# A fixed order of 32 experts, and the order of a second attention's weights, in a two-block transformer kernel

## The chip, the cores and the metric

The kernel runs as one program on one core of a Trainium2 chip. The metric is device time in microseconds for one execution of the whole program; times of several executions are given as their median. The core has TensorE (in the profile PE for its matmuls, PEld for its weight loads), VectorE (DVE), ScalarE (ACT), GpSimd (POOL) and SyncE (SP), which here issues nearly all DMAs from one in-order queue. Sixteen DMA engines move the data.

## The reference, cut to what matters

Two transformer blocks over 256 tokens of width 1024, in float32. The first block has a mixer (short convolution, gated delta rule, stick-breaking attention) and a feed-forward layer. The second block is conditioned by a vector c, and ends in a mixture of 32 experts, of which each token takes four:

```python
mod = silu(c) @ w_ada + b_ada                       # 1024 x 6144
sh1, sc1, gt1, sh2, sc2, gt2 = split(mod, 6)
h = rms_norm(x, g_pre_mix) * (1 + sc1) + sh1
dq, dk, dv, nq, nk, nv = split(h @ w_in)            # two attentions
mix = concat(diff_attention(dq, dk, dv), neighbourhood_attention(nq, nk, nv)) @ w_out
x = x + gt1 * rms_norm(mix, g_post_mix)
h2 = rms_norm(x, g_pre_ffn) * (1 + sc2) + sh2
f = moe_ffn(h2, ...)                                # 32 experts, top 4, w1 1024x2048, w2 1024x1024 each
x = x + gt2 * rms_norm(f, g_post_ffn)
```

## The kernel before

**Weights.** The dense weights are 67 slabs of one megabyte, numbered in the order of use; w_ada is 24 more ("a" slabs), eight for each third of the modulation. `WS` merges the two lists: `ADA_AT[j]` says ahead of which dense slab the a slab j is loaded. A slab goes into one of six half buffers (three pairs, `w_pair`); the string `PLACES` names the half for each slab of `WS`. `load_slabs` issues slab n once slab n - 6 and the last holder of its half have been read. A dense slab counts as read when ScalarE and VectorE have split it into a high and a low part (`split`, at most four half slabs ahead of use); an a slab when its four matmuls have been written. When the dense list is at its end, each pair of halves, once both are read, becomes one buffer for an expert slab.

**Second attention.** Its twelve slabs are: values of the differential heads (vd, two slabs), keys and queries of differential heads 0 to 3 (one slab each), values of the neighbourhood heads (vn, two slabs), keys and queries of neighbourhood heads 0 to 3 (one each); w_out has four. A host function `pack` puts them into this order. On the chip the stage is written as generators: `head(i)` for i from 0 to 7 (scores, softmax, transposes, mix with the values), `shifts()` for the small vectors, and `projections2()`, which runs `values("vd")`, `keys(0)` to `keys(7)` and `values("vn")`, then the first six of eight w_out products. A planner, `weave`, takes from each generator what TensorE does next and a cost in us, and so fixes the order of instructions when the program is built; `yield 0, 3.0` lets three us of the planner's time go by. `ada(2)` is the last third of the modulation: eight rounds of matmuls into bank acc00, a copy by ScalarE, four transposes, an addition. `shifts()` computes from it the vectors that scale the router's weights. `values` uses banks acc00 and acc01, `head` uses acc10 and acc11, and the w_out products use all four.

**Experts.** The router's top four give counts; experts 0 and 1 are fixed as ranks 0 and 1, the others are sorted by count, largest first. Rank r has a fixed capacity `CAPS[r]` in tokens: 64 for ranks 0 and 1, 128 for 2 and 3, 96 for 4 to 7, 64 for 8 to 17, 32 for 18 to 31. `ORDER` lists the ranks as they are computed; position p is the p-th entry. An expert is six slabs of two megabytes: four of w1, two of w2. There are ten buffers for them, and `load_m` refills buffers in the order of the loads: load n goes into the buffer of load n - 10, when that one and all ahead of it are released. Position p has loads 6p to 6p + 5.

A capacity is cut into blocks of 64 and 32 tokens: 128 is two of 64, 96 is one of 64 and one of 32. For each block TensorE runs `first_rounds` (w1, L1725; two rounds for a block of 64, one for 32), and then `second` (transposes L1745, w2 at L1768 for 64 and L1763 for 32). Slabs are released by the last block of an expert alone. In between stand the gathering of the next expert's tokens (L1683, L1694, L1709) and the addition of the expert before (`combine`, L1791). The last position takes the expert alone with the closing norm (`finish`) behind it.

```python
def free_m(keys):
    for k in keys:
        del m_slab[k]
        m_freed.add(m_num.pop(k))
    while state["freed"] in m_freed:
        load_m(state["next"], m_pool[state["freed"]])
        state["next"] += 1
        state["freed"] += 1
```

Of the kernel before, what the change touches and what calls it, by code (L numbers as in the profile page):

```python
# [21 lines left out]
P = 128  # L22
# [12 lines left out]
NA = 3  # L35


PLACES = "250134250134250134254012543254301254301254301254301243025432154201534201453120345012345"

TURNS = "FABADACCEG"  # L40
NS = len(TURNS)
# [7 lines left out]

FIRST = 2  # L50
CAPS = [64] * 2 + [128] * 2 + [96] * 4 + [64] * 10 + [32] * 14
ORDER = [0, 1, 8, 18, 9, 2, 26, 10, 3, 27, 11, 4, 28, 12, 5, 19, 13, 6, 29, 14, 7, 20, 15, 30, 21, 16, 22, 17, 23, 24, 25,
         31]


N_DENSE = 67
ADA_AT = [14] * 3 + [20] * 5 + [38, 41, 44, 47] + [-1] * 4 + [54] * 2 + [55] * 2 + [56] * 2 + [57] * 2
WS = [w for i in range(N_DENSE + 1) for w in
      [("a", j) for j in range(24) if ADA_AT[j] == i] + ([("s", i)] if i < N_DENSE else [])]
WS_DENSE = [i for i, w in enumerate(WS) if w[0] == "s"]  # L60
# [106 lines left out]
def kernel(ctx: ExitStack, tc: tile.TileContext, x_in, cols_in, rows_in, const_in, cona_in, conb_in, rpb_in,  # L167
# [82 lines left out]
    def load_all(names):  # L250
        for m in range(NS):
            if TURNS[m] in names:
                load_m(m)
# [26 lines left out]
    def col(name, i=None, n=1):  # L280
        a, b = COLS[name]
        t = cols
        if a >= NKEPT:
            t, a, b = cols_mix[0], a - NKEPT, b - NKEPT
        return t[:, a:b] if i is None else t[:, a + i:a + i + n]
# [97 lines left out]
    with sx:  # L383
# [105 lines left out]
        def ada(i, b=None):  # L489

            b = bank() if b is None else b
            for k in range(KC):
                s = WS_ADA[state["ada"]]
                state["ada"] += 1
                w = s_slab[s].rearrange("p (g n) -> p g n", g=4)
                for g in range(4):
                    nc.tensor.matmul(b[32 * g:32 * (g + 1), :], silc[:, k:k + 1].to_broadcast([P, 32]), w[:, g, :],
                                     start=(k == 0), stop=(k == KC - 1))
                slab_read(s)
                if k < KC - 1:  # L500
                    yield 0.94, 0
            r = hp.tile([P, 512], F32, name="adar", tag="wide")
            nc.scalar.activation(r, b, AF.Copy)
            yield 0.94, 1.0
            t = bank()
            for j in range(4):
                nc.tensor.transpose(t[:, j * P:(j + 1) * P], r[:, j * P:(j + 1) * P], ident)
            nc.vector.tensor_tensor(mod[:, 16 * i:16 * (i + 1)].rearrange("p (g j) -> p j g", g=4),
                                    t.rearrange("p (j g r) -> p j g r", j=4, g=4)[:, :, :, 0],
                                    col("b_ada")[:, 16 * i:16 * (i + 1)].rearrange("p (g j) -> p j g", g=4),  # L510
                                    op=OP.add)
            yield 0.3, 0
# [467 lines left out]
        with ExitStack() as s2:  # L980
# [190 lines left out]
            with ExitStack() as s3:  # L1171
# [32 lines left out]
                def values(name):  # L1204
                    t = act.tile([P, 2, 512], F32, name=name)
                    b = [psa.tile([P, 512], F32, name=f"acc0{c}") for c in range(2)]
                    for s in range(2):
                        us = [[u.rearrange("p (k n) -> p k n", k=2) for u in un] for un in units(2)]
                        for c in range(2):
                            for k in range(4):  # L1210
                                kc = 4 * s + k
                                wh, wl = us[k // 2]
                                tok_mm(lambda c, h: b[c], kc, hTh, hTl, wh[:, k % 2, :], wl[:, k % 2, :], kc == 0,
                                       kc == KC - 1, (c,))
                                if k % 2:
                                    if c and k == 1:
                                        split_ahead(3)
                                    yield flush() + [("p", 1.3)]
                    nc.scalar.activation(t[:, 0, :], b[0], AF.Copy)
                    nc.vector.tensor_copy(t[:, 1, :], b[1])  # L1220
                    vs[name] = t

                def keys(i):
                    while i - count["scores"] >= 3:
                        yield 0, 0.1
                    pair = []
                    for n, s in (("k", 1.0), ("q", 1.0 if i < 4 else 0.125)):
                        b = bank()
                        yield from proj_steps(b)
                        t = wk.tile([P, T], F32, name=n + "2", bufs=3)  # L1230
                        nc.scalar.activation(t, b[:, 0:T], AF.Copy, scale=s)
                        pair.append(t)
                        yield [("p", 0.65)]
                    kq[i] = pair
                    if i in (1, 2):
                        nc.scalar.activation(x[:, i - 1, :], x[:, i - 1, :], AF.Copy, scale=r[:, i - 1, 0:1])
                        yield [("A", 1.06)]
                    if i >= 4:
                        window(i - 4)
                        yield [("V", 1.9)]  # L1240
# [122 lines left out]
                def shifts():  # L1363

                    yield 0, 1.0
                    yield from fill
                    yield 0, 4.0
                    b = bank()
                    for k in range(KC):
                        nc.tensor.matmul(b[:, 0:NE], mod[:, 24 + k:25 + k].to_broadcast([P, P]),  # L1370
                                         col("router")[:, k * NE:(k + 1) * NE], start=(k == 0), stop=(k == KC - 1))
                    nc.vector.tensor_add(brow, b[:, 0:NE], row("b_router"))
                    yield 1.0, 4.0
                    gg = small.tile([P, KC], F32, name="gg")
                    nc.vector.tensor_mul(gg, mod[:, 16:24], col("g_post_mix"))
                    for _ in row_steps(gg, grow, hp.tile([P, 4, P], F32, name="diag", tag="wide")):
                        yield 0, 1.5
                    while "ada" not in vs:
                        yield 0, 0.1
                    nc.vector.tensor_mul(gg2, mod[:, 40:48], col("g_post_ffn"))  # L1380

                    nc.vector.scalar_tensor_tensor(gs, mod[:, 32:40], 1.0, col("g_pre_ffn"), op0=OP.add, op1=OP.mult)
                    wr = col("router").rearrange("p (k e) -> p k e", k=KC)
                    nc.vector.tensor_tensor(wr, wr, gs[:, :, None].to_broadcast([P, KC, NE]), op=OP.mult)
# [2 lines left out]

                def projections2():
                    yield from values("vd")
                    fill = ada(2, psa.tile([P, 512], F32, name="acc00"))  # L1390
                    for i in range(8):
                        if i == 4:
                            yield from fill
                            vs["ada"] = True
                            yield from values("vn")
                        yield from keys(i)
                        if i < 4:
                            yield next(fill)
                            yield next(fill)
                    load_all("B")  # L1400
                    while count["scores"] < 8:
                        yield 0, 0.1
                    acc.extend(new_acc())
                    for kc in range(KC - LAST):
                        while count["joined"] <= kc:
                            yield 0, 0.1
                        if "D" not in pools and (count["turned"] == 8 or kc == KC - LAST - 1):
                            while count["turned"] < 8:
                                yield 0, 0.1
                            s4.close()  # L1410
                            pools["D"] = ctx.enter_context(tc.tile_pool(name="slabsD", bufs=1, side="right",
                                                                        reuse_waits="tile"))
                            load_all("D")
                        wh, wl = unit()
                        tok_mm(lambda c, h: acc[c][h], kc, yTh, yTl, wh, wl, kc == 0, False)
                        yield flush() + [("p", 2.6)]
                    while count["joined"] < KC:
                        yield 0, 0.1
# [585 lines left out]
def pack(inp):  # L2004
# [17 lines left out]
    def ada(i):  # L2022
        return [wa[k * P:(k + 1) * P, 2048 * i:2048 * (i + 1)] for k in range(KC)]
# [10 lines left out]
        return ([rows_k(w2[512 * i:512 * (i + 1), v:v + 512]) for i in range(2)]  # L2034
                + [chunk_cols(w2, (k + h * P, q + h * P)) for h in range(4)])

    S += attn(512, 0, 1024) + attn(2048, 1536, 2560)
    S += by2(f("w_out_2")[0])
    S = {"s": S, "a": ada(0) + ada(1) + ada(2)}
    assert len(S["s"]) == N_DENSE  # L2040
# [60 lines left out]
```

## Time and profile before

| | |
|---|---|
| median of 3 runs | 1496.65 us (1492.77 to 1497.12) |
| the profiled execution | 1493.93 us |
| its span, first to last instruction | 1492.1 us |
| mean granted TensorE clock | 0.969 |
| TensorE matmuls busy | 1370.7 us, 92% of the span |
| expert slabs | 192 loads of 2048 KB |

A busy TensorE is an average over stages with different limits: the expert loads are 192 x 2.097 = 402.7 MB of the 504 MB that are read in all. The span is what the trace shows; the execution's time has 1.8 us more around it.

### The profile page before, as it was taken

What the parts mean: (1) busy time and instruction counts of PE and PEld (TensorE: products, weight loads), DVE (VectorE), ACT (ScalarE), POOL (GpSimd) and SP (SyncE); (2) the same over time, 40 slices, a digit from 0 to 9 for tenths busy, and PEclk for the clock granted to TensorE, in tenths of its full rate; (3) what the DMA queues carried; (4) which work ended last, traced back from release to release, by engine and by line L of the source; (5) the groups of instructions that cost most, each with busy time, mean ns of one, the idle gap of its engine ahead of it and who ended that gap; (6) DMA issues with size and microseconds to landing.
All of it is one profiled execution on the core that took longest, in us unless ns stands there. A gap on an engine that the chain in (4) does not pass through costs nothing.

```text
span 1492.1 us, 21744 instructions
## 1 busy us (share of the span) xinstructions
PE 1370.7 (92%) x8859; PEld 736.1 (49%) x8863; DVE 546.6 (37%) x1258; ACT 455.9 (31%) x979; POOL 55.6 (4%) x31
## 2 busy tenths in 40 slices
PE   7999999999899999999999999999999987887674
PEld 6899789998678753333333333333333322222121
DVE  4755678776757841222122122112112111111112
ACT  5564465555556641111111111112111111101111
POOL 2322010000000000000000000000000000000000
PEclk9999999999999999999999999999999998989887
DMA  8322586656774599999899899999999999999994
GB/s 314 113 92 107 186 330 248 258 200 228 260 277 174 179 390 402 424 427 421 345 429 417 346 427 417 426 426 427 428 427 428 427 427 427 428 427 427 428 427 186
DMA packets 43433, 506.66 MB, mean 340 GB/s; under 512 B 5024, under 2 KB 5280, under 8 KB 6880
## 3 DMA queue, kind: packets, MB, share of 16 engines
q1 hardware_dynamic: 42464, 503.49, 82.5%
q10 hardware_dynamic: 864, 1.72, 0.4%
q8 instruction: 72, 1.18, 0.3%
q14 instruction: 33, 0.27, 0.0%
HBM read 504.14 MB, written 1.05 MB: 339 GB/s over the span
## 4 chain that ended last, share of the span: by engine, by line
PE 74%; DMA 17%; ACT 4%; DVE 3%; issue 1%; POOL 0%; SPq 0%; ACTq 0%; DVEq 0%; POOLq 0%
PE mm L1725 23%; DMA w<-in_we 16%; PE mm L447 15%; PE mm L1768 9%; PE acc L1791 4%; PE mm L1683 3%; PE mm L1763 3%; PE acc L481 3%; PE acc L482 3%; PE acc L483 3%; DMA w<-in_ws 1%; PE mm L824 1%; ACT aT L1746 1%; PE mm L1694 1%; PE mm L1730 1%
## 5 line engine op out<-in xcount | busy, mean ns | idle before, releaser
L1725 PE MATMUL mm<-w,xT 128*64 128x512 f32 (+1 forms) x2432 | 449.4, 642 | 56.3 <-DMA w<-in_we 56.0
L1725 PEld LDWEIGHTS mm<-w,xT 128*64 128x64 f32 (+1 forms) x2432 | 134.1, 131 | 354.2 <-issue 279.6
L1734 DVE TENSOR_SCALAR h<-mm 128x256 f32<-128x256 f32 x58 | 24.6, 425 | 714.8 <-PE mm L1730 714.8
L447 PE MATMUL mm<-hT,u 128*128 128x256 f32 x2064 | 263.5, 287 | 1.4 <-DVE hT L436 0.6
L447 PEld LDWEIGHTS mm<-hT,u 128*128 128x128 f32 x2064 | 254.1, 193 | 12.8 <-issue 8.4
L1735 ACT ACTIVATE a<-h 128x256 f32<-128x256 f32 x58 | 24.2, 417 | 506.0 <-DVE h L1734 506.0
L408 DVE TENSOR_TENSOR u<-w,u 128x1024 fp32r<-128x1024 f32 x115 | 145.5, 1270 | 67.3 <-ACT u L403 67.3
L403 ACT ACTIVATE u<-w 128x1024 fp32r<-128x1024 f32 x134 | 139.9, 1056 | 34.0 <-PE acc L483 23.9
L1768 PE MATMUL mm<-w,aT 128*64 128x512 f32 x640 | 143.2, 600 | 5.3 <-ACT aT L1746 5.3
L1768 PEld LDWEIGHTS mm<-w,aT 128*64 128x64 f32 x640 | 44.5, 138 | 91.2 <-issue 81.0
L1773 ACT ACTIVATE y<-mm 128x512 f32<-128x512 f32 x38 | 22.7, 597 | 208.6 <-PE mm L1768 139.8
L1763 PE MATMUL mm<-w,aT 128*32 128x512 f32 x576 | 65.5, 595 | 9.9 <-ACT aT L1746 9.9
L1683 PE MATMUL mm<-x,S 128*32 128x256 f32 (+1 forms) x448 | 57.4, 463 | 2.5 <-DVE S L1670 2.5
L408 POOL TENSOR_TENSOR u<-w,u 128x1024 fp32r<-128x1024 f32 x19 | 46.8, 2465 | 330.5 <-PE mm L306 201.4
L1063 DVE SCALAR_TENSOR_TENSOR fcv<-mm,cols,fcv 128x255 f32<-128x255 f32 x88 | 42.3, 481 | 22.9 <-ACT fcv L1060 21.4
L1701 ACT ACTIVATE xT<-mm,mod,gs 128x64 f32<-128x64 f32 (+1 forms) x152 | 46.6, 386 | 2.1 <-PE mm L1694 1.5
L1703 DVE TENSOR_SCALAR xT<-mm,gs,mod 128x64 f32<-128x64 f32 (+1 forms) x152 | 38.7, 321 | 3.0 <-PE mm L1694 3.0
L1763 PEld LDWEIGHTS mm<-w,aT 128*32 128x32 f32 x576 | 16.8, 109 | 46.5 <-issue 31.1
L1683 PEld LDWEIGHTS mm<-x,S 128*32 128x32 f32 (+1 forms) x448 | 18.7, 119 | 39.6 <-issue 33.1
L1926 POOL TENSOR_TENSOR fs<-fs,x 128x512 f32<-128x512 f32 x1 | 1.3, 1259 | 946.9 <-ACT fr L314 946.9
L1060 ACT ACTIVATE fcv<-mm,cols 128x256 f32<-128x256 f32 x44 | 20.7, 471 | 50.8 <-PE mm L447 50.8
L481 PE MATMUL acc<-u,gh 128*128 128x512 f32 x88 | 34.9, 397 | 0.0
(546 smaller groups left out, 1374.5 us busy)
## 6 DMA issues: line engine op xcount, KB each, us to landing
w<-in_we SPq DMA_DIRECT2D x192, 2048.0 KB, 23.3
w<-in_ws SPq DMA_DIRECT2D x90, 1024.0 KB, 5.3
nb<-in_rpb SPq DMA_DIRECT2D x4, 512.0 KB, 7.7
x<-in_x SPq DMA_DIRECT2D x2, 512.0 KB, 6.1
w<-in_ws SPq DMA_DIRECT2D x2, 512.0 KB, 7.5
bt<-in_b SPq DMA_DIRECT2D x3, 256.0 KB, 8.5
out<-fs SPq DMA_DIRECT2D x3, 256.0 KB, 2.1
grow<-in_wf ACTq DMA_DIRECT2D x1, 512.0 KB, 4.9
```

The lines of the kernel that those rows point to most:

```text
L403: nc.scalar.activation(hi, raw, AF.Copy)
L408: eng.tensor_tensor(lo, raw, hi, op=OP.subtract)
L447: nc.tensor.matmul(b[:, 0:T], w[:, k, :], h[:, k, :], start=(n == 0), stop=(n == 3 * KC - 1))
L481: nc.tensor.matmul(o, th[:, kc, t], wh[:, w], start=first, stop=False)
L482: nc.tensor.matmul(o, th[:, kc, t], wl[:, w], start=False, stop=False)
L483: nc.tensor.matmul(o, tl[:, kc, t], wh[:, w], start=False, stop=last)
L1683: nc.tensor.matmul(b[p * tb:(p + 1) * tb, 0:n], S[:, c, p * tb:(p + 1) * tb], x[:, c, p * n:(p + 1) * n], start=(c == 0), stop=(c == 1))
L1701: nc.scalar.activation(dst, src, AF.Identity, scale=gs[:, kc:kc + 1], bias=mod[:, 24 + kc:25 + kc])
L1725: nc.tensor.matmul(b[p * tb:(p + 1) * tb, :], xT[:, k, q * tb:(q + 1) * tb], w1(p * nr + rd, kc // 4)[:, kc % 4, :], start=(kc == 0), stop ...
L1763: nc.tensor.matmul(b[p * tb:(p + 1) * tb, :], aT[:, 0, j, p0 * tb:(p0 + 1) * tb], w2(bi)[:, j, h * 512:(h + 1) * 512], start=(bi == 0), st ...
L1768: nc.tensor.matmul(b[p * tb:(p + 1) * tb, :], aT[:, rd, j, p0 * tb:(p0 + 1) * tb], w2(bi)[:, j, p * 512:(p + 1) * 512], start=(bi == 0 and ...
L1791: nc.tensor.matmul(acc[c][h], lhsT, rhs, start=False, stop=False, skip_group_check=True)
```

## The change

Three constants and four lines of the second attention. `ORDER` puts ranks with capacity 32 and 64 in front. Position by position the capacities were 64, 64, 64, 32, 64, 128, 32, 64, 128, 32, 64, 96, 32, 64, 96, 32, 64, 96, 32, 64, 96, 32, 64, 32, 32, 64, 32, 64, 32, 32, 32, 32, and become 64, 64, 32, 32, 64, 64, 64, 32, 128, 32, 32, 32, 96, 32, 64, 64, 96, 32, 96, 32, 64, 32, 96, 64, 64, 32, 128, 32, 32, 64, 64, 32. In the second attention vn comes after `keys(1)` instead of after `keys(3)`; the eight rounds of `ada(2)` come one after each of `keys(2)` to `keys(7)` and two at the end, and its transposes and addition move into `shifts()`, three us of planner's time behind. The a slabs move in the list accordingly. `PLACES` names other halves; up to slab 65 each slab follows the same one as before in its half, only the numbers of the halves differ.

```diff
-PLACES = "250134250134250134254012543254301254301254301254301243025432154201534201453120345012345"
+PLACES = "531240531240531240530125304530412530412530412530412504153045230512340512340521435012345"
-ORDER = [0, 1, 8, 18, 9, 2, 26, 10, 3, 27, 11, 4, 28, 12, 5, 19, 13, 6, 29, 14, 7, 20, 15, 30, 21, 16, 22, 17, 23, 24, 25,
-         31]
+ORDER = [0, 1, 18, 19, 8, 9, 10, 20, 2, 21, 22, 23, 4, 24, 11, 12, 5, 25, 6, 26, 13, 27, 7, 14, 15, 28, 3, 29, 30,
+         16, 17, 31]
-ADA_AT = [14] * 3 + [20] * 5 + [38, 41, 44, 47] + [-1] * 4 + [54] * 2 + [55] * 2 + [56] * 2 + [57] * 2
+ADA_AT = [14] * 3 + [20] * 5 + [38, 41, 44, 47] + [-1] * 4 + [58, 59, 60, 61, 62] + [63] * 3
...
                     while "ada" not in vs:
                         yield 0, 0.1
+                    yield 0, 3.0
+                    yield from vs["ada"]
                     nc.vector.tensor_mul(gg2, mod[:, 40:48], col("g_post_ffn"))
...
                     yield from values("vd")
-                    fill = ada(2, psa.tile([P, 512], F32, name="acc00"))
                     for i in range(8):
-                        if i == 4:
-                            yield from fill
-                            vs["ada"] = True
+                        if i == 2:
                             yield from values("vn")
+                            fill = ada(2, psa.tile([P, 512], F32, name="acc00"))
                         yield from keys(i)
-                        if i < 4:
-                            yield next(fill)
+                        if i >= 2:
                             yield next(fill)
                     load_all("B")
+                    yield next(fill)
+                    next(fill)
+                    yield 0.94, 0.3
+                    vs["ada"] = fill
...
-    S += attn(512, 0, 1024) + attn(2048, 1536, 2560)
+    a1, a2 = attn(512, 0, 1024), attn(2048, 1536, 2560)
+    S += a1[:4] + a2[:2] + a1[4:] + a2[2:]
```

## Rows read from the trace of the kernel before

**Rows 1.** The page's slices: bytes moved, 40 equal parts of the span.

```profile
GB/s 314 113 92 107 186 330 248 258 200 228 260 277 174 179 390 402 424 427 421 345 429 417 346 427 417 426 426 427 428 427 428 427 427 427 428 427 427 428 427 186
```

**Rows 2.** The chain of waits in order of time (start, us, what), its last part.

```profile
1215.75 39.07 DMA w<-in_we
...
1461.98 4.87 PE mm L1725 x25
```

**Rows 3.** Windows: stretch, length, busy per engine, PEclk, DMA share, GB/s.

```profile
700.00:720.00 20.00, 19.75 (x108) 6.89 (x105) 6.32 (x20) 3.64 (x11) 0.00 (x0) 1.00 1.00 419
720.00:740.00 20.00, 19.62 (x118) 6.36 (x118) 0.00 (x0) 2.34 (x5) 0.00 (x0) 1.00 0.69 274
...
800.00:820.00 20.00, 19.75 (x108) 7.03 (x106) 5.12 (x16) 3.22 (x10) 0.00 (x0) 1.00 0.99 410
820.00:840.00 20.00, 19.61 (x130) 6.53 (x126) 1.18 (x3) 3.11 (x8) 0.00 (x0) 1.00 0.69 273
...
880.00:900.00 20.00, 20.00 (x144) 6.63 (x141) 3.30 (x9) 1.22 (x3) 0.00 (x0) 1.00 0.99 407
...
920.00:1460.00 540.00, 471.70 (x2842) 154.92 (x2834) 94.06 (x304) 78.48 (x217) 0.00 (x0) 0.94 1.01 427
```

**Rows 4.** The chain of waits: first w1 matmuls of positions 0, 1, 2, 5, 6, 7, 11, 12.

```profile
547.71 7.09 PE mm L1725 x32
...
580.74 7.02 PE mm L1725 x32
...
607.43 6.87 PE mm L1725 x32
...
685.38 6.87 PE mm L1725 x32
...
735.09 7.00 PE mm L1725 x64
...
751.29 7.02 PE mm L1725 x32
...
877.62 6.87 PE mm L1725 x32
...
916.79 7.00 PE mm L1725 x64
```

**Rows 5.** Expert loads: seventh, 31st, up to the 45th (that one's landing), up to 77th.

```profile
L246 SPq DMA_DIRECT2D w<-in_we x1: 327/327/327, 530.3 to 530.3; - x1
...
DMA to landing us min/median/max: 8.5/8.5/8.5
...
L246 SPq DMA_DIRECT2D w<-in_we x1: 332/332/332, 645.9 to 645.9; - x1
...
DMA to landing us min/median/max: 16.2/16.2/16.2
...
L246 SPq DMA_DIRECT2D w<-in_we x45: 327/333/1222, 389.1 to 730.0; - x45
...
DMA to landing us min/median/max: 9.0/9.0/9.0
...
L246 SPq DMA_DIRECT2D w<-in_we x77: 327/333/1222, 389.1 to 896.3; - x77
```

**Rows 6.** TensorE's waits, 546 to 660: for whom, us in total, times, longest.

```profile
PE mm L1683 <- DVE S L1670: 1.8, 1, 1.8
```

**Rows 7.** Windows of the second attention, columns as in rows 3.

```profile
395.00:531.50 136.50, 130.88 (x855) 105.50 (x854) 91.75 (x189) 79.40 (x188) 2.59 (x1) 0.99 0.64 238
480.00:500.00 20.00, 19.83 (x160) 18.28 (x160) 19.24 (x49) 14.39 (x39) 0.00 (x0) 1.00 0.39 131
```

**Rows 8.** TensorE's waits, 394 to 531.

```profile
PE mm L507 <- ACT adar L503: 4.2, 2, 3.1
```

**Rows 9.** TensorE's timeline at 453.67: the transposes, idle time before them in brackets.

```profile
453.67 0.66 PE L507 MATMUL mm<-cst,adar 128*128 128x128 f32 x4 [1.06 <-ACT adar L503]
```

**Rows 10.** One window, columns as in rows 3.

```profile
1220.00:1250.00 30.00, 21.54 (x116) 5.57 (x120) 3.51 (x12) 3.34 (x9) 0.00 (x0) 0.79 1.01 428
```

## The prediction

> **What bounds the kernel now.** I read the page's slices first: from the fifteenth slice to the last but one 390 to 429 GB/s are moved, but for two dips, to 345 and 346 [rows 1]. The chain of waits, read backwards from the end, is one stretch of expert-slab DMA from 1215.75 to 1461.98 and then a tail of matmuls and vector work; before 1215.75 it runs on TensorE [rows 2]. So two limits follow each other, and what joins them is the slab stream: it has no gap after 920 (540 us at 427 GB/s, [rows 3]), so every microsecond that it lost before then is still missing at the end, although TensorE is idle by then. The windows tell where it lost them. At 427 GB/s a 2,097 KB slab takes 4.91 us; a window's deficit is its length times (427 - rate) / 427. That gives 0.4 us in 700:720, 7.2 in 720:740, 0.8 in 800:820, 7.2 in 820:840 and 0.9 in 880:900, together 16.5 us [rows 3].
>
> Why it lost them: ten buffers are refilled in strict order, so load n waits until slab n - 10 is released. An expert is six slabs, 29.4 us of stream. TensorE's time for one, from its first L1725 group to the next expert's, is 26.7 us for a capacity of 64 (580.74 to 607.43), 49.7 for 128 (685.38 to 735.09), 16.2 for 32 (735.09 to 751.29) and 39.2 for 96 (877.62 to 916.79) [rows 4]. Call lag the time from the landing of an expert's first slab to its first matmul. Against 29.4 us the lag changes by -2.7 for 64, +20.3 for 128, -13.2 for 32 and +9.8 for 96; it can't fall below about zero, where TensorE waits for slabs.
>
> A 128 expert has two blocks and releases slabs only with the second. In position 5 its fifth slab (the 35th of all) was released 44.6 us after its start, when the 45th load was issued at 730.0; that load landed 9.0 us later, so 4.1 us lie between issue and the 4.9 us of transfer [rows 4, 5]. The stream has no gap if this release comes 4.1 us before the fourteenth landing counted from the expert's first, that is 13 x 4.9 - 4.1 = 59.6 us after the first landing. So a 128 expert stalls the stream when it starts with a lag over 59.6 - 44.6 = 15.0 us. Here the first slab landed at 645.9 + 16.2 = 662.1 and the lag was 23.3: a stall of 8.3 by this rule, 7.2 by the window. For a 96 expert the first slab binds: released 896.3 - 877.62 = 18.7 us after the start, limit 9 x 4.9 - 4.1 - 18.7 = 21.3 us [rows 4, 5]. Every stall of the window view sits at a 128 or a 96 that was reached with too much lag.
>
> **The change, part by part.** (1) *Order of ranks.* Work and bytes are the same: every rank once. What moves is the lag. Position 1 starts at 580.74, its first slab having landed at 530.3 + 8.5 = 538.8: lag 41.9 [rows 4, 5]. Positions 0 and 1 stay. Before, only one 32 lies ahead of the first 128, and the lag there is still 23.3. After, positions 2 to 7 hold 32, 32, 64, 64, 64, 32. From 41.9, position 1 takes 2.7, the two 32s 13.2 each, less 3 us that I allow for the routing work which the code puts behind positions 2 and 3 (an estimate: TensorE waited 1.8 us for VectorE there, [rows 6], and has some small matmuls), three 64s 2.7 each and the 32 of position 7 13.2: 41.9 - 2.7 - 26.4 + 3 - 8.1 - 13.2 = -5.5, so zero is reached before position 8, where the first 128 stands. It starts with lag 0; TensorE then is paced by the landings through the first four slabs (18.2 us instead of 14.2), which counts as a lag of 4. Limit 15: 11 us to spare, no stall. After it the lag is 24; a 32 or 64 with one block releases at once, and three 32s bring it to zero. Each later 96 is reached after a 32, or after two 64s behind a 32, with a lag of 0 to 4 against 21; the other 128, position 26, comes after 64, 64 and 32 at zero. So the whole 16.5 us should go. Lower bound of the gain 9 us (one 128 still costs its stall), upper 18.5 (a little more if position 1, which gathers for a 32 next, releases earlier). I take 16.5.
>
> The end: the last expert is rank 31 before and after, and the 30 us behind 1461.98 [rows 2] hang on its fourth slab. The two 64s ahead need 26.7 of 29.4 us, so TensorE waits by then in either order: no cost, hidden by the stream; rival E has what it is without that cover.
>
> (2) *Values early, third modulation late.* The same matmuls, in another order. TensorE is busy 130.88 of the 136.5 us from 395 to 531.5 [rows 7], so the stage is bound by its own matmuls and their sum does not change. It was idle 4.2 us for the transposes of the modulation, waiting for ScalarE's copy, in two places, 3.1 us in the longer one [rows 8]; the 1.06 us one, at 453.67, is that of the third modulation [rows 9]. The new text lets 3 us go by (in the planner's time) ahead of these transposes, so that wait should go: -1.06. The eight rounds of modulation matmuls (0.94 us each in the planner's list), which need nothing of VectorE, now stand between the neighbourhood heads, where VectorE is busy 19.24 of 20 us [rows 7]: some tenths more. Against it, the first output product needs the bank that the modulation held, so it waits for the same ScalarE copy, with exponentials queued ahead of it; behind it on TensorE stand all output products. Bounds: gain at most the 5.6 us of idleness less the 3.1 that stay, 2.5; loss at most one more wait like the longer, 3.1. I take -1.5, nearer to the wait that is seen to go.
>
> (3) *Slots and queue.* The stream is at 0.64 of its capacity in this stage [rows 7], so one-megabyte slabs in another order cost nothing while each is issued a key step ahead. On SP's queue the last modulation slabs now release the first pair, so the second expert load goes out later, behind the output weights; the seventh load lands at 538.8 and the first expert starts at 547.71 [rows 4, 5], so some 9 us cover it. If that cover were gone, the start of the experts would move one for one.
>
> **Sum.** -16.5 - 1.5 = -18.0 us on the span of 1492.1: 1474.1. The profiled execution took 1493.93, 1.8 over its span: 1475.9. The median of the runs, 1496.65, is 2.7 over that execution: **1478.6**, say 1478.5.
>
> **Rivals.** *A, the forecast* (0.74): 1474 to 1483.
>
> *B, stalls come back at other experts* (0.12). TensorE would wait for slabs from position 8 on instead of from 1215, and where it waits like that, in 1220:1250, the granted clock was 0.79 in the mean [rows 10], so for some 42% of the time at the lower level, 1.2 GHz. The Trainium skill's page "TensorE: Matmul & The Clock Gate", section "HAM oscillation — how this bites in real kernels", states that an engine which waits for DMA between bursts begins each burst at half clock; the fall to 0.79 agrees. By the row alone: at 0.79 a 128 takes 49.7 / 0.79 = 62.9 us, 13.2 more, 2 over the 11 to spare; for the two of them 4 us, 1482.5. A clock below that stalls each by up to the 8 of before, and the 96s a little: up to 1493. Against it: a 128 has four rounds without a wait once its first four slabs are there.
>
> *C, the attention loses* (0.08): a wait in front of the output products of 3 to 6 us beyond my value: 1482 to 1487 with the stalls gone.
>
> *D, no effect* (0.03): the stream's dips are the memory's and not the buffers'; 1493 to 1499. Against it: the rule gives their places.
>
> *E, slower* (0.03): the two 64s at positions 29 and 30 fall behind. They run at the end, with nothing to absorb a lag: at clock g they take 26.7 / g, and decide from g = 0.91 on. At 0.79 they take 33.8, 4.4 over each, 9 us in all; it ends slower than before only if g stays near 0.65 through both, 11.7 over each: 1502. No row of this trace is so low over 30 us.
>
> **Chances.** A difference under 0.3% (4.5 us) can't be told from none. A, B's better part and C give faster: 0.92; the rest of B and D same: 0.05; E slower: 0.03. A lies within 1471 to 1487, with C and the lower third of B: about 0.84.
>
> **What would show it.** Right: no window of 20 us between 640 and the last landing below 420 GB/s; TensorE waits for expert slabs from about 740; the last L1725 wait ends 18 us earlier; slab DMA in the chain well before 1215; no wait at L507 in the second attention but the first. Wrong: a dip near 790 to 820 or 1320 to 1350 (the 128s), TensorE still in a 64 when the last slab lands, or an attention stage longer than 136.5 us. The number is wrong by just as much as the first expert starts earlier or later than I have it.

## The result, and the profile after

The changed kernel takes 1477.88 us (median of four runs, 1477.23 to 1479.49) beside 1495.02 us for the kernel before in the same rounds: ratio 0.9889, 95% interval [0.9875, 0.9903], about 17 us faster. Forecast were 1478.5 and "faster". The profiled execution took 1478.14 us, its span is 1476.3 instead of 1492.1, and the mean granted clock is 0.984 instead of 0.969. Lines from the experts' part on carry a number that is three higher than before (L1725 is now L1728, L1683 is L1686, L1768 is L1771).

The page of the kernel after, its slices:

```profile
span 1476.3 us, 21754 instructions
...
PEclk9999999999999999999999999999999999999998
...
GB/s 317 115 87 92 209 321 230 272 215 231 238 151 229 279 352 389 430 427 427 427 428 428 426 427 428 427 429 427 426 428 427 427 428 426 427 428 426 428 429 172
```

The two dips of [rows 1] are gone; from the seventeenth slice on no slice but the last is below 426. Windows of the kernel after, columns as in [rows 3]:

```profile
700.00:720.00 20.00, 19.69 (x108) 6.94 (x106) 6.44 (x22) 3.23 (x10) 0.00 (x0) 1.00 1.00 427
720.00:740.00 20.00, 14.59 (x80) 3.60 (x80) 0.00 (x0) 1.79 (x3) 0.00 (x0) 0.83 1.00 426
...
800.00:820.00 20.00, 19.47 (x166) 6.86 (x166) 3.50 (x12) 3.62 (x10) 0.00 (x0) 1.00 1.01 428
820.00:840.00 20.00, 18.06 (x147) 5.34 (x136) 4.83 (x18) 4.00 (x12) 0.00 (x0) 1.00 1.01 425
880.00:900.00 20.00, 18.59 (x136) 6.47 (x134) 5.12 (x16) 3.23 (x10) 0.00 (x0) 1.00 1.01 427
395.00:531.50 136.50, 131.66 (x856) 105.50 (x855) 92.08 (x190) 80.14 (x189) 2.58 (x1) 0.99 0.63 236
1283.50:1336.60 53.10, 49.04 (x252) 16.91 (x256) 8.32 (x24) 5.95 (x17) 0.00 (x0) 1.00 1.01 428
750.70:803.30 52.60, 49.01 (x256) 16.73 (x256) 8.33 (x24) 6.40 (x17) 0.00 (x0) 1.00 1.01 428
640.00:1450.00 810.00, 731.51 (x4308) 245.73 (x4308) 150.64 (x485) 123.32 (x337) 0.00 (x0) 0.99 1.01 427
```

The two windows that held 274 and 273 GB/s [rows 3] hold 426 and 425, and the stream runs at 427 GB/s for 810 us. 750.70:803.30 and 1283.50:1336.60 are the two experts of capacity 128 (positions 8 and 26). In 720:740 the roles are turned round: the stream is full, and TensorE is idle for 5.4 of 20 us. The chain of waits, in order of time (start, us, what):

```profile
547.59 7.09 PE mm L1728 x32
...
579.16 8.71 PE mm L1728 x32
...
625.77 7.00 PE mm L1728 x64
...
641.80 7.02 PE mm L1728 x32
648.86 37.72 DMA w<-in_we
686.74 38.88 DMA w<-in_we
725.74 39.06 DMA w<-in_we
764.84 3.65 PE mm L1728 x16
...
803.53 6.87 PE mm L1728 x64
811.02 33.62 DMA w<-in_we
844.76 39.07 DMA w<-in_we
...
1368.22 39.03 DMA w<-in_we
1407.37 39.04 DMA w<-in_we
1446.45 4.64 PE mm L1728 x25
```

Before, slab DMA entered the chain in 1215.75 [rows 2]; now it carries it from 648.86, with stretches on TensorE in between (764.84 to 811.02 is the first 128), in which the stream has no gap. The last wait for a slab ends at 1446.45 instead of 1461.98, 15.5 us earlier, and what follows takes 29.8 us instead of 30.1. Nearly all of the 15.8 us on the span lie there. From each load's issue and its time to landing, the 192nd slab lands at 1456.15 instead of 1471.67.

How the first 128 is met, on TensorE's timeline (idle time before in brackets):

```profile
750.72 3.65 PE L1728 MATMUL mm<-w,xT 128*64 128x512 f32 x16
755.05 3.65 PE L1728 MATMUL mm<-w,xT 128*64 128x512 f32 x16 [0.69 <-DMA w<-in_we]
...
760.05 3.65 PE L1728 MATMUL mm<-w,xT 128*64 128x512 f32 x16 [1.12 <-DMA w<-in_we]
764.84 3.65 PE L1728 MATMUL mm<-w,xT 128*64 128x512 f32 x16 [1.14 <-DMA w<-in_we]
```

It is paced by landings through its first four slabs, as forecast, and starts 0.6 us after its first slab (landed 750.1). It releases its fifth slab 48.4 us after its start; from 44.6 and the lag counted as 4 I had 48.6.

What the clock did with the earlier waits, TensorE by form of matmul over the whole expert part, two rows of the kernel after and the second one's counterpart before:

```profile
L1728 PE MATMUL mm<-w,xT 128*64 128x512 f32 x1280 | 288.8, 598 | 30.2 <-DMA w<-in_we 29.6 <-DVE xT L1706 0.3
L1728 PE MATMUL mm<-w,xT 128*32 128x512 f32 x1152 | 144.4, 624 | 26.3 <-DMA w<-in_we 26.3
...
L1725 PE MATMUL mm<-w,xT 128*32 128x512 f32 x1152 | 163.0, 690 | 49.0 <-DMA w<-in_we 49.0
```

The sum of the waits for slabs is as large as before, 55.9 us beside 56.0. Before, they came after 1215.75, 49.0 us of them ahead of the w1 matmuls of blocks of 32 tokens, which averaged 690 ns; spread over 810 us they leave these at 624. No time came of it: the stream sets the pace either way.

### The profile page after: what moved, and what is told of

Its sections match the earlier page's. It is cut to its first block, busy times and chain, and to the rows that moved or that the text cites. A ratio compares the mean times of both kernels' runs of the same rounds, so it can differ in the third digit from the quotient of the medians.

```text
span 1476.3 us, 21754 instructions
## 1 busy us (share of the span) xinstructions
PE 1353.6 (92%) x8859; PEld 730.1 (49%) x8863; DVE 546.5 (37%) x1258; ACT 456.6 (31%) x979; POOL 55.6 (4%) x31
## 4 chain that ended last, share of the span: by engine, by line
PE 53%; DMA 40%; DVE 3%; ACT 3%; issue 1%; SPq 0%; POOL 0%; ACTq 0%; DVEq 0%; POOLq 0%
DMA w<-in_we 39%; PE mm L447 16%; PE mm L1728 12%; PE mm L1771 5%; PE acc L481 3%; PE acc L482 3%; PE acc L483 3%; PE acc L1794 1%; PE mm L1686 1%; PE mm L1766 1%; DMA w<-in_ws 1%; PE mm L824 1%; DVE u L408 1%; PE mm L497 1%; PE acc L1254 1%
## 5 line engine op out<-in xcount | busy, mean ns | idle before, releaser
L1728 PE MATMUL mm<-w,xT 128*64 128x512 f32 (+1 forms) x2432 | 433.2, 611 | 56.5 <-DMA w<-in_we 55.9
L1728 PEld LDWEIGHTS mm<-w,xT 128*64 128x64 f32 (+1 forms) x2432 | 129.2, 126 | 343.9 <-issue 254.1
L1737 DVE TENSOR_SCALAR h<-mm 128x256 f32<-128x256 f32 x58 | 24.6, 425 | 699.3 <-PE mm L1733 699.3
L447 PE MATMUL mm<-hT,u 128*128 128x256 f32 x2064 | 264.3, 287 | 2.4 <-ACT hT L434 0.9
L447 PEld LDWEIGHTS mm<-hT,u 128*128 128x128 f32 x2064 | 253.7, 193 | 16.1 <-issue 10.3
L1771 PE MATMUL mm<-w,aT 128*64 128x512 f32 x640 | 141.7, 595 | 5.8 <-ACT aT L1749 5.6
L1771 PEld LDWEIGHTS mm<-w,aT 128*64 128x64 f32 x640 | 44.2, 137 | 90.5 <-issue 80.0
L1686 PE MATMUL mm<-x,S 128*32 128x256 f32 (+1 forms) x448 | 56.7, 460 | 2.4 <-DVE S L1673 2.4
L1686 PEld LDWEIGHTS mm<-x,S 128*32 128x32 f32 (+1 forms) x448 | 18.5, 119 | 39.8 <-issue 30.4
L481 PE MATMUL acc<-u,gh 128*128 128x512 f32 x88 | 34.9, 397 | 0.0
```

The source lines that it names most:

```text
L447: nc.tensor.matmul(b[:, 0:T], w[:, k, :], h[:, k, :], start=(n == 0), stop=(n == 3 * KC - 1))
L481: nc.tensor.matmul(o, th[:, kc, t], wh[:, w], start=first, stop=False)
L1686: nc.tensor.matmul(b[p * tb:(p + 1) * tb, 0:n], S[:, c, p * tb:(p + 1) * tb], x[:, c, p * n:(p + 1) * n], start=(c == 0), stop=(c == 1))
L1728: nc.tensor.matmul(b[p * tb:(p + 1) * tb, :], xT[:, k, q * tb:(q + 1) * tb], w1(p * nr + rd, kc // 4)[:, kc % 4, :], start=(kc == 0), stop ...
L1771: nc.tensor.matmul(b[p * tb:(p + 1) * tb, :], aT[:, rd, j, p0 * tb:(p0 + 1) * tb], w2(bi)[:, j, p * 512:(p + 1) * 512], start=(bi == 0 and ...
```

## The experiments

The kernel before took 1493.83 us (median) beside runs 1 to 4, 1492.65 beside 5, 6, 7 and 9, and 1494.7 beside 8 and 10, which ran once each. "Late landings" are landings that follow the one before by more than the usual 4.90 us, worked out from issue and time to landing of each load.

**1. The order alone.** The kernel before, with nothing but the new order.

```diff
-ORDER = [0, 1, 8, 18, 9, 2, 26, 10, 3, ...
+ORDER = [0, 1, 18, 19, 8, 9, 10, 20, 2, ...
```

> The kernel before with the new order of ranks alone. Theory (lag): the order carries all of the gain, 15 to 17 us under before; no 20 us window between 640 and the last slab under 420 GB/s, and the second attention as long as before. Rival (attention): one to two us of the gain came from the attention stage, so this stays at 13 to 15 us under before.

Measured: 1478.07 us, ratio 0.9897 [0.9883, 0.9912], the same as the full change; the last slab lands at 1455.50.

**2. The attention alone.** The changed kernel with the old order.

```diff
-ORDER = [0, 1, 18, 19, 8, 9, 10, 20, 2, ...
+ORDER = [0, 1, 8, 18, 9, 2, 26, 10, 3, ...
```

> The changed kernel with the old order of ranks: the second attention's part alone. Theory: within 1 us of before, since TensorE's wait for the modulation's copy (1.06 us) is paid back by more switches between kinds of matmuls; the two dips of the slab stream (at 720:740 and 820:840 before) are there, 14 to 17 us together. Rival: the wait that went is worth its 1 to 1.5 us in the total.

Measured: 1493.28 us, ratio 0.9996 [0.9986, 1.0006]. The attention part is worth nothing that the total tells from no change. Both dips are back in its windows, at the same places:

```profile
720.00:740.00 20.00, 19.62 (x124) 6.15 (x124) 0.00 (x0) 2.34 (x5) 0.00 (x0) 1.00 0.72 292
...
820.00:840.00 20.00, 19.62 (x130) 6.95 (x130) 2.98 (x10) 4.11 (x11) 0.00 (x0) 1.00 0.73 297
```

**3 and 4. A 128 reached with more lag.** If the limit of 15.0 us is right, the first 128 may move up to position 4 and not to position 3.

```diff
-ORDER = [0, 1, 18, 19, 8, 9, 10, 20, 2, 21, ...
+ORDER = [0, 1, 18, 19, 2, 8, 9, 10, 20, 21, ...   # run 3
+ORDER = [0, 1, 18, 2, 19, 8, 9, 10, 20, 21, ...   # run 4
```

> The changed kernel with the first 128 expert (rank 2) moved from position 8 to position 4. Theory (a 128 stalls the stream when it starts with a lag over 15 us): the lag at position 4 is 9 to 13 us (9.1 in the changed kernel, and position 3 gathers for two blocks instead of one), so there is no stall and the time is that of the changed kernel, 0 to 1 us over it. Rival (the stream needs the 128s late, whatever the lag): 7 us more.

> The changed kernel with rank 2 at position 3. Theory: the lag there is 22.8 us in the changed kernel and about 4 more with two blocks to gather for, 12 over the limit of 15: stalls of 8 to 14 us in all, the last slab lands as much later, and the time is 8 to 14 us over the changed kernel. Rival (dips that are the memory's own): no difference to rank 2 at position 4.

Measured: at position 4, 1478.69 us, ratio 0.9896 [0.9881, 0.991]: the 128 starts with a lag of 11.6, and no window is below 424 GB/s. At position 3, 1488.15 us, ratio 0.9957 [0.9943, 0.9972]: lag 23.8, where some 27 was expected, and 9.5 us more than run 3. Windows of the kernel with the 128 at position 3:

```profile
640.00:660.00 20.00, 20.00 (x110) 7.08 (x106) 5.70 (x16) 2.99 (x9) 0.00 (x0) 1.00 0.97 392
660.00:680.00 20.00, 18.72 (x96) 6.91 (x98) 1.69 (x7) 2.81 (x8) 0.00 (x0) 1.00 0.70 283
680.00:700.00 20.00, 19.47 (x144) 6.66 (x138) 3.64 (x12) 3.23 (x9) 0.00 (x0) 1.00 0.98 399
...
820.00:840.00 20.00, 12.43 (x62) 2.88 (x63) 0.00 (x0) 0.00 (x0) 0.00 (x0) 0.66 1.01 428
```

The dip moved with the expert, from 720 to 660. Later TensorE waits a lot for slabs, and none of it brings the lost time back.

**5. A 128 late.** The second one goes from position 26 to position 30.

```diff
-... 15, 28, 3, 29, 30, 16, 17, 31]
+... 15, 28, 29, 30, 16, 17, 3, 31]
```

> The changed kernel with the second 128 expert (rank 3) moved from position 26 to position 30, the last but one. Theory: its lag of about 24 us is no longer taken back; the last expert starts 24 us behind its first slab instead of waiting for its fourth, so TensorE ends 11 to 14 us later and the time is 11 to 14 us over the changed kernel, with no dip in the slab stream. Rival (the end is bound by the stream, and what TensorE does there is hidden): no difference.

Measured: 1494.34 us, ratio 1.001 [0.9997, 1.0022]: the whole gain is lost, some 16 us, a little over what was expected. The last slab lands at 1455.43, as early as in the changed kernel; the last expert's matmuls start at 1460.66 instead of 1437.1. A window and a step of the chain of this run (its L1727 is L1728 of the changed kernel):

```profile
1430.00:1460.00 30.00, 28.57 (x131) 10.12 (x128) 3.78 (x10) 4.76 (x13) 0.00 (x0) 1.00 0.71 301
```

```profile
1460.66 7.00 PE mm L1727 x64
```

Here the stream has run out of loads while TensorE is still busy: what bounds the end has changed from DMA to TensorE. Position 30 took 56.4 us, not 49.7, since it was paced by landings first.

**6 and 7. Shorter experts.** Both kernels without the additions of 29 experts' results to the sum, so that TensorE has one group of 1.92 us less for each block.

```diff
-                combine(*pend.pop(0), into_acc)
+                p_ = pend.pop(0)
+                if pos >= 30:
+                    combine(*p_, into_acc)
```

> The changed kernel without the matmuls that add the outputs of 29 of the 32 experts (1.9 us of TensorE for each block, some 70 us in all): that part of the result is left out. Theory (slab stream from position 2 on): nearly the time of the changed kernel, 0 to 3 us less, since only positions 1 to 3 still delay the stream. Rival (TensorE's work in the experts sets the time): tens of us less.

> The kernel before with the same matmuls left out. Theory (lag): position 5 starts with 7.6 us less lag and releases its fifth slab 1.9 us sooner, which brings it just under the limit, position 8 likewise; the dips go and the time falls to that of the changed kernel, 14 to 19 us under before. Rival (the dips are the memory's own at these loads): no difference to before.

Measured: from the changed kernel 1478.95 us, ratio 0.9905 [0.9882, 0.9929], no difference: TensorE's work no longer counts there. From the kernel before 1488.5 us, ratio 0.9963 [0.9949, 0.9977]: 4.2 us between the medians and 5.5 by the ratio, where 14 to 19 were expected. That was a miss. The lag at position 5 fell by 4.0 us and not by 7.6, and 2.4 of the 4.0 were there at position 1 already (39.5 instead of 41.9), ahead of the first addition. The fifth slab was released 44.0 us after position 5's start, 0.75 sooner and not 1.9. TensorE's waits from 580 to 740 in this run:

```profile
PE mm L1745 <- ACT xT L1701: 3.0, 4, 0.8
PE mm L1745 <- DVE a L1738: 2.3, 2, 1.1
...
PE mm L1745 <- DVE h L1736: 0.7, 2, 0.4
```

None of these three is among the waits of the kernel before in that stretch. Five additions of 1.92 us went, 9.6 us, and 6.0 us of waits came: the additions had stood where TensorE would else have waited ahead of the hidden layer's transposes (L1745), half of it for ScalarE's copies of the gathered tokens and half for VectorE's part of the activation. Behind the longest of these waits the 32 matmuls of L1763 took 5.34 us instead of 3.64, in a stretch (635 to 652) with a granted clock of 0.89. So from position 1's first matmuls to position 6's the way is only 2.5 us shorter, 151.8 instead of 154.3. The two windows with dips:

```profile
720.00:740.00 20.00, 18.49 (x124) 6.14 (x120) 1.98 (x6) 4.00 (x11) 0.00 (x0) 1.00 0.84 338
...
800.00:820.00 20.00, 18.45 (x92) 6.41 (x88) 3.72 (x13) 3.55 (x11) 0.00 (x0) 1.00 0.82 349
```

The miss still serves the rule, because it gave a lag in between. Capacities of 128 in these traces, in order of lag; the last column adds up the landings that are over 0.5 us late among the loads that refill the expert's six slabs. Those not listed start with a lag of 2.6 or less; behind four of them, in runs 8 and 9, one landing is 1.4 to 1.5 us late, of the kind told of at the end.

| kernel, position | lag at its start, us | stall by the rule (lag - 15.0) | sum of late landings behind it, us |
|---|---|---|---|
| after, 26 | 0.1 | none | none |
| after, 8 | 0.6 | none | none |
| run 3, 4 | 11.6 | none | none |
| run 7, 5 | 19.2 | 4.2 | 3.1 |
| run 2, 5 | 21.6 | 6.6 | 6.8 |
| before, 5 | 23.1 | 8.1 | 8.5 |
| before, 8 | 23.2 | 8.2 | 8.2 |
| run 2, 8 | 23.3 | 8.3 | 8.3 |
| run 7, 8 | 23.7 | 8.7 | 6.1 |
| run 4, 3 | 23.8 | 8.8 | 8.7 |

The limit lies between 11.6 and 19.2, and the size is right to within 1.1 us but for one of 2.6. In run 7 the terms of the rule are others: with the release at 44.0 us and the fifth load's 7.6 and 7.8 us from issue to landing instead of 9.0, the limit is some 16.9 and the two stalls come out at 2.3 and 6.8.

**8. The modulation's rounds in pairs.** To test why the attention gained so little: the eight rounds go in pairs behind every second key step, which makes fewer changes from one kind of matmul to another.

```diff
-                        if i >= 2:
+                        if i in (3, 5, 7):
+                            yield next(fill)
                             yield next(fill)
```

> The changed kernel with the modulation's rounds in pairs, after keys 3, 5 and 7, instead of one after each of keys 2 to 7. In the trace of the changed kernel a matmul ahead of a switch between kinds takes 0.20 to 0.22 us to the next start and not 0.12, and leaving a modulation round takes 0.52. Theory (switches pay back the wait that went): three groups less, 0.5 to 0.9 us less from the first key matmul to the warm-up behind the last output product (117.3 us in the changed kernel, 117.8 before). Rival (the stage is paced by VectorE's splits): no difference, or longer.

Measured, one run: 1478.56 us. Waits of TensorE from 394 to 531 that only this kernel has, and its key and value projections (L447) from 413 to 531.5:

```profile
PE mm L1334 <- ACT e L1316: 1.8, 1, 1.8
...
PE mm L1327 <- ACT e L1316: 0.2, 1, 0.2
```

```profile
L447 PE MATMUL mm<-hT,u 128*128 128x256 f32 x384 | 50.1, 287 | 0.0
```

The same row before, and after:

```profile
L447 PE MATMUL mm<-hT,u 128*128 128x256 f32 x384 | 49.9, 287 | 0.0
...
L447 PE MATMUL mm<-hT,u 128*128 128x256 f32 x384 | 52.1, 289 | 0.0
```

So the projections got their time back, and a wait of 2.0 us for ScalarE's exponentials took it: the stage became 118.0 us instead of 117.3, where 116.4 to 116.8 were expected.

**9. The bias matmuls later.** The chain of the changed kernel has 3.63 us of bias matmuls (L1883) between positions 0 and 1. Here they stand behind the first rounds of position 1.

```diff
+        if pos == 1:
+            for c in range(2):
+                for h in range(2):
+                    nc.tensor.matmul(acc[c][h], gateT[:, c * P:(c + 1) * P], b2[h], start=True, stop=False,
...
-        if pos == 0:
-            for c in range(2):
-                for h in range(2):
...
```

> The changed kernel with the matmuls of the experts' output biases (L1883, 3.6 us of TensorE) moved from in front of position 1's first matmuls to behind its first rounds. Theory: slabs 6 to 9 are released 3.6 us sooner, at the one place where the stream still waits (lag 39.5 us against a limit of 36 for a 64); loads 16 to 19 land 1 to 3 us sooner and so does everything behind: 1 to 3 us under the changed kernel. Rival (the delay is taken back by the following slabs, or moves to the next release): no difference.

Measured: 1476.97 us, ratio 0.9892 [0.9874, 0.991]: no difference, a miss. Position 1 starts at 576.4 instead of 579.1, but position 2 at 609.7 instead of 607.6, and the 25th slab lands at 634.16 instead of 632.62. These are read from the profiled run, the slowest of the six (1479.88 us). The delay was moved, not removed.

**10. Without the delay.** The three us of planner's time ahead of the modulation's transposes are taken out.

```diff
-                    yield 0, 3.0
```

> The changed kernel without the three microseconds of planner time ahead of the modulation's transposes. Theory: TensorE waits there (L507) for ScalarE's copy again, 0.5 to 1.5 us, and the stretch from the first key matmul to the warm-up grows from 117.3 us by as much. Rival (other work of the planner's comes first anyway): no wait, no difference.

Measured, one run: 1479.3 us; the stage takes 118.05 us instead of 117.29. Its waits of TensorE from 394 to 531:

```profile
PE mm L507 <- ACT adar L503: 3.5, 2, 3.1
PE acc L481 <- DVE s L1266: 0.8, 1, 0.8
```

Of the 1.06 us wait, 0.35 is back: the delay removed that rest, and the later place of the whole modulation the greater part.

No run is measurably faster than the change; runs 1, 3, 6 and 9 equal it.

## Why the prediction was right, point by point

**What bounds the kernel: right.** The stream's losses before 920 stood in the end time, and nothing after brought them back; run 4 shows it once more. Where the stream is whole, TensorE's work is free (run 6).

**Order of ranks: right, forecast -16.5, measured -15.5.** Run 1 has the whole gain and run 2 none of it. Five late landings of before, behind positions 5, 8 and 11, add up to 17.8 us and are gone. Not all of it is gained: summed over the 182 landings behind the tenth, the stream's loss against 4.897 us for each fell from 24.6 to 9.0 us, 15.6. Elsewhere the stream of before lost 24.6 - 17.8 = 6.8 us; the 9.0 that the changed kernel loses hold four single late landings of 1.1 to 1.3 us (loads 55, 91, 126 and 165), the first of them in the stretch where before had its stalls. The lags along the way: 41.9 was forecast at position 1 and 39.5 is seen, 36.5 at position 2, 22.8, 9.1, 6.4, 3.6, 3.6, and 0.6 at position 8 where zero was forecast; then 23.9, forecast 24.

**Attention: mis-sized, forecast -1.5.** The term's first part held: the waits for the transposes' copy went from 4.2 us in two places [rows 8] to 3.1 in one, here from TensorE's waits from 394 to 531 after:

```profile
PE mm L507 <- ACT adar L503: 3.1, 1, 3.1
...
PE acc L481 <- DVE s L1266: 0.6, 1, 0.6
```

But the stage, from its first key or value product to the work behind the last output product, went only from 117.76 to 117.29 us (117.32 in run 2, which has the same attention). Counted from each start to the next start, the groups that fell gave 2.9 us (the modulation's with its wait 0.81, the softmax's transposes 0.74, scores and others the rest), and those that rose took 2.4: the projections L447 1.41, the output products 0.43, two small ones 0.58. The step that failed is "the same matmuls, in another order", costed at no more than tenths: there are 68 changes of kind now instead of 60, and 35 of the projections' matmuls instead of 22 were followed by 0.14 us or more, from start to start, where 0.122 is usual. Of the 35, 21 are the first behind a change and 14 the last ahead of one; nine other last ones have the usual 0.12, so what was expected of run 8, which speaks of the matmul ahead of a change, names the smaller part. Run 8 shows the link for L447: with 58 changes, 22 of its matmuls are followed by 0.14 us or more. Of the 0.47 us that remained, 0.1 arrived at the seventh expert load (530.17 instead of 530.29).

**Slots and queue, tail: right.** Tenth landing 555.92 instead of 555.78; behind the last slab 20.1 us instead of 20.4.

**The number was nearer than its terms.** On the span, -18.0 was forecast and -15.8 measured. The 2.7 us that I added from the profiled execution to the median were too many as well: the changed kernel's median is 0.3 below its profiled execution. Two errors of 2.2 and 3.0 us nearly cancel.

**Rivals.** B had the right danger and the wrong size: TensorE did wait from position 8 on, but with pauses of 0.5 to 1.2 us ahead of each slab the granted clock stayed at 1.00, its upper level of 2.4 GHz, through both 128s; it was 0.83 in the window 720:740. There, on TensorE's timeline of the kernel after, and in a window behind the long wait:

```profile
725.66 3.63 PE L1728 MATMUL mm<-w,xT 128*32 128x512 f32 x30 [0.29 <-DMA w<-in_we]
...
735.46 4.93 PE L1728 MATMUL mm<-w,xT 128*32 128x512 f32 x24 [3.85 <-DMA w<-in_we]
...
735.40:738.00 2.60, 2.54 (x12) 0.60 (x16) 0.00 (x0) 0.00 (x0) 0.00 (x0) 0.50 0.98 416
```

Thirty matmuls take 3.63 us; behind a wait of 3.85 us 24 of the same take 4.93, the first twelve at a granted clock of 0.50, the lower level of 1.2 GHz. The Trainium skill's rule of bursts that begin at half clock after a DMA wait (page "TensorE: Matmul & The Clock Gate", section "HAM oscillation — how this bites in real kernels") agrees with the last two of these lines. The waits of 0.5 to 1.2 us, to which I had carried it, left the clock up. C: the wait in the output products (L481, for VectorE) is 0.6 us instead of 0.4, not 3 to 6. D is refuted by runs 3 and 4: the dip goes to 660 with a 128 that is reached with much lag, and stays away from one with little. E didn't happen with two 64s at the end (positions 29 and 30 start with a lag of 0.1, and the last with 5.4), but what it feared, a lag at the end that nothing takes back, is real: run 5 puts a 128 there, and the gain is gone.

## What to carry to other kernels

With a ring of buffers that is refilled in strict order, follow the lag (landing to first use) and not the busy share: an item that holds its buffers long stalls the stream only if it starts late, so clear the lag with short items first, and keep long ones out of the last positions, where nothing takes their lag away again. Lost transfer time is final once the transfers bound the end, and work taken off the compute engine is then worth nothing (run 6). When you cost a matmul group that you would move or remove, ask what it covers: 9.6 us of additions removed gave 2.5, and 1.06 us of wait removed was mostly eaten by more frequent changes of kind.

## What the runs showed of the hardware

- One core read 427 GB/s from memory for 810 us on end (window 640:1450).
- A change from one kind of matmul to another cost TensorE time here. In the second attention of the kernel after, L447's matmuls stand in 23 groups: the first of a group was followed by 0.20 to 0.22 us in 19 of them (0.52 in two), the last by 0.21 us or more in 14, the others by 0.122.
- Once the stream is full, a landing is late by 1.1 to 1.5 us about every 35 loads (55, 91, 126, 165 after; 60, 96, 130, 169 in run 9), or two in that stretch by 0.4 to 1.1 (before; run 5). What causes it stays open: no run was made for it.
